# A hybrid attention and SSD layer on one core: the first phase in emission order, with the tokens' norms from squared rows

## The chip, the cores and the metric

The kernel runs on one core of one Trainium2 chip. A core has TensorE (matmuls), VectorE, ScalarE, GpSimd and SyncE; SyncE's queue (SP) issues every transfer of this kernel. The metric is the device time of one execution in microseconds (us), the median of several runs.

## The reference

One layer over 2048 tokens of 1024 features and 256 memory tokens, in float32:

```python
memn = rms_norm(mem, norm_mem_w)
hn = rms_norm(h, norm_in_w[layer])
proj = hn @ w_in[layer]
q, k, v, g_attn, z, xbc, dt_raw, q_mem, g_mem = jnp.split(proj, splits, axis=-1)
...                                   # rotary on q and k
att = window_attention(q, k, v, attn_sink[layer]).reshape(bsz, l, ATT_W)
...                                   # convolution, SSD scans in both directions, gate, norm
mkv = memn @ w_mem_kv[layer]
mk, mv = jnp.split(mkv, 2, axis=-1)
...                                   # attention of q_mem over mk, mv; gates
h = h + mixed @ w_out[layer]
return rms_norm(h, norm_out_w)        # rms_norm: y = x * rsqrt(mean(x*x) + 1e-6) * w
```

The first phase of the kernel, which the change edits, computes the memory's keys and values (`mkv`) and, for the last tokens, `hn` and from it `k` and `v`.

## The kernel before

Every float32 product is made from three matmuls of a faster 32-bit type: each operand is split into a high half (`xh`, `wh`, `memh`: a cast on ScalarE) and a low half (`xl`, `wl`, `meml`: a subtraction on VectorE, for a few tiles on GpSimd). `split3` issues high x high, high x low and low x high into one bank. A weight tile is 128 x 1024; `load_w` loads it into a staging tile `ws` (two buffers) and splits it into `wh` and `wl` (three buffers each).

The 2048 tokens are worked on in four chunks of 512, last chunk first, each with 128 tokens ahead of it, so 640 columns (`XW`). The first phase goes like this:

- memory: eight blocks of 128 features x 256 tokens are scaled and split (`memh`, `meml`). `mem_keys(hd, w)` makes the keys of one of four heads (24 matmuls of 256 columns); `mem_values(k2, w)` adds a quarter of the features to the values (12 matmuls of 512 columns) in two banks `pss`. The sums of squares go through `rstd_sq` (matmuls with a column of ones, then a power on GpSimd), `diag` (the norm of each token on a diagonal) and `rows_bc` (a matmul with ones, which spreads them over all rows; ScalarE copies the result).
- `mem_keys_out` multiplies keys by the norm (`kf`, VectorE), splits them into a tile "mk" and stores it in `mk_d`. The values are scaled from their banks, split (low half on GpSimd) into tiles "mk" too, and stored in `mv_d`. "mk" has two buffers.
- tokens: `xT` is loaded in eight blocks of 128 x 640. ScalarE squares them, VectorE adds the eight squares, `rstd_sq` sums them over the partitions. `prep_x` scales each block by weight and norm (VectorE), casts (ScalarE) and subtracts (VectorE).
- `keys` for the last chunk: two halves of 320 tokens. First both products with weight `wa` (banks `pa`), then for each half the product with `wb` (bank `pb`) and `rope`, in which VectorE multiplies `pa` and `pb` by the tables of `tables` (tile "tab", one buffer), adds, and ScalarE and VectorE split; two stores to `k_d`. Then `values`: five blocks of 24 matmuls of 272 columns. `pa`, `pb`, the blocks of `values` and the memory products share the three banks of `ps_pj`.

The order of instructions on TensorE is the order in which the program emits them. On the other engines and in SP's queue a scheduler orders them at compile time by readiness in its own model and by priority (`high_priority` raises it); each engine then runs its list in order, and an instruction that waits for a semaphore holds up all behind it. The lines that matter are L177 (all matmuls), L195 and L196 (cast and subtraction of `split`), L202 (weight loads), L361 (scaling of tokens), L371 (table), L862 and L864 (`kf` and its store), L241 to L243 (`rope`), L385 (store of keys), L850 (power) and L910:

```python
        for u in range(2):
            nc.sync.dma_start(mv_d[u, m], as32(mvs[u]))   # L910, m = 0 and 1; keys() comes next
```

## Time and profile before

| | |
|---|---|
| median of 3 runs | 1847.41 us (1845.33 to 1850.26) |
| the profiled execution's own time | 1848.8 us |
| its span, first to last instruction | 1847.1 us |
| TensorE busy, share of the span | 95% |
| mean granted clock of TensorE in it | 0.985 of full speed |

Times in the rows are us from the start of the span unless marked ns. A row of the waits says which engine and line waited for which, in total, how often and the longest. In a row of the timeline stand start, duration, engine, line, operation, output and inputs, and in brackets how long the engine sat idle before and until what. PEld is the loading of weights into TensorE, which overlaps PE, its matmuls.

### The profile page before, as it was taken

Reading aid. Unit: us, or ns where it says so; the run is one execution under the profiler, and the core shown is the slowest. Engines: PE = TensorE matmul, PEld = TensorE weight load, DVE = VectorE, ACT = ScalarE, POOL = GpSimd, SP = SyncE. Lnnn points to the kernel's source line nnn. Section 1 sums busy time; section 2 is a strip of 40 time slices with the busy share of each in tenths; the row PEclk is TensorE's granted clock in tenths of the full one; section 3 lists DMA queues with packets and bytes.
Section 4 is the critical chain, followed back from the end, with each engine's and each line's share of the span. In section 5 each row is a group of like instructions: output and inputs, shape, how many; then the busy total and the mean of one; then the engine's idle time right before and its main releaser. Section 6 shows DMA issues by size and latency. Waiting matters only on the chain. (4 is left out here: it accounts for less than half of the span.)

```text
span 1847.1 us, 26627 instructions
## 1 busy us (share of the span) xinstructions
PE 1755.7 (95%) x9242; PEld 1426.0 (77%) x9242; DVE 1179.9 (64%) x2681; ACT 921.4 (50%) x1985; POOL 260.3 (14%) x253
## 2 busy tenths in 40 slices
PE   7889999999799999999999989999998999999998
PEld 6878878877578787777778877778776777787886
DVE  7466666688576667778666777977677543443443
ACT  6237645664665566657555654656566411111121
POOL 1000000012200000121000002210111133333321
PEclk9989999999899999999999989999998999999999
DMA  7666364578653854776475466673658586566553
GB/s 237 211 197 187 123 214 146 152 241 244 210 169 122 268 165 150 240 245 206 142 211 161 133 205 195 190 214 118 197 179 265 165 251 182 164 180 180 171 176 120
DMA packets 264422, 347.59 MB, mean 188 GB/s; under 512 B 29536, under 2 KB 172000, under 8 KB 264288
## 3 DMA queue, kind: packets, MB, share of 16 engines
q1 hardware_dynamic: 264288, 345.90, 61.1%
q8 instruction: 73, 1.20, 0.3%
q14 instruction: 61, 0.50, 0.1%
HBM read 254.34 MB, written 91.49 MB: 187 GB/s over the span
## 5 line engine op out<-in xcount | busy, mean ns | idle before, releaser
L177 PE MATMUL pj<-xh,wh 128*128 128x512 f32 (+2 forms) x1296 | 506.6, 391 | 2.8 <-ACT xh L195 1.0
L177 PE MATMUL pj<-xl,wh 128*128 128x512 f32 (+2 forms) x1296 | 494.0, 381 | 4.8 <-DVE xl L196 4.8
L177 PE MATMUL pj<-xh,wl 128*128 128x512 f32 (+2 forms) x1296 | 494.7, 382 | 0.9 <-DVE wl L196 0.8
L196 DVE TENSOR_TENSOR wl<-ws,wh 128x1024 fp32r<-128x1024 f32 (+2 forms) x175 | 212.3, 1214 | 117.3 <-ACT wh L195 112.9
L177 PEld LDWEIGHTS pj<-xh,wl 128*128 128x128 f32 x1296 | 246.0, 190 | 46.9 <-DVE wl L196 2.7
L177 PEld LDWEIGHTS pj<-xh,wh 128*128 128x128 f32 x1296 | 246.7, 190 | 41.9 <-issue 3.7
L177 PEld LDWEIGHTS pj<-xl,wh 128*128 128x128 f32 x1296 | 246.8, 190 | 40.7 <-DVE xl L196 5.9
L195 ACT CAST wh<-ws 128x1024 fp32r<-128x1024 f32 (+2 forms) x175 | 180.0, 1029 | 179.3 <-PE pj L177 127.6
L546 DVE CUSTOM_DVE_ANT_0 pm<-s,band,sink 128x384 f32<-128x384 f32 (+1 forms) x256 | 150.3, 595 | 48.3 <-PE s L177 46.4
L554 ACT ACTIVATE pm<-pm,mx 128x385 f32<-128x385 f32 (+1 forms) x256 | 151.2, 595 | 55.5 <-DVE mx L552 55.5
L177 PE MATMUL pj<-woh,mxh 128*128 128x512 f32 x416 | 169.1, 407 | 0.0
L177 PE MATMUL pj<-woh,mxl 128*128 128x512 f32 x416 | 164.2, 395 | 0.0
L177 PE MATMUL pj<-wol,mxh 128*128 128x512 f32 x416 | 164.1, 394 | 0.0
L648 POOL TENSOR_TENSOR b<-nat,win 128x256 f32<-128x256 f32 x64 | 43.3, 697 | 841.2 <-ACT nat L632 841.2
L558 ACT ACTIVATE pm<-pm,den 128x384 f32<-128x384 f32 (+1 forms) x256 | 133.5, 595 | 6.9 <-DVE den L556 6.8
L572 ACT COPY pt<-t 128x512 f32<-128x512 f32 x120 | 69.4, 583 | 103.6 <-PE t L181 103.3
L195 ACT CAST mxh<-mxl 128x512 fp32r<-128x512 f32 x64 | 39.5, 617 | 162.8 <-DMA mxl<-mix_d 105.7
L181 PE MATMUL t<-ident,pm 128*128 128x128 f32 x736 | 103.8, 276 | 11.6 <-ACT nat L632 6.7
L181 PEld LDWEIGHTS t<-ident,pm 128*128 128x128 f32 x736 | 86.5, 142 | 34.6 <-ACT nat L632 7.6
L177 PE MATMUL s<-khh,qs 128*128 128x384 f32 (+1 forms) x256 | 94.7, 370 | 18.3 <-DVE mx L546 13.8
L484 DVE SCALAR_TENSOR_TENSOR cu<-raw,cw,cu 128x512 f32<-128x512 f32 (+2 forms) x128 | 99.3, 776 | 3.3 <-ACT cu L482 2.0
L177 PE MATMUL o<-pt,vg 128*64 128x256 f32 x736 | 93.8, 388 | 1.6 <-DVE dq L425 0.7
(222 smaller groups left out, 2842.8 us busy)
## 6 DMA issues: line engine op xcount, KB each, us to landing
ws<-in_w_in_dram SPq DMA_DIRECT2D x152, 512.0 KB, 4.2
q_d<-rt SPq DMA_DIRECT2D x32, 512.0 KB, 4.3
qs<-q_d SPq DMA_DIRECT2D x32, 512.0 KB, 6.1
fb<-f_d SPq DMA_DIRECT2D x32, 512.0 KB, 4.4
mxl<-mix_d SPq DMA_DIRECT2D x64, 256.0 KB, 4.1
mix_d<-ao SPq DMA_DIRECT2D x64, 128.0 KB, 3.5
xc<-xbc_d SPq DMA_DIRECT2D x32, 256.0 KB, 3.7
st_d<-carry SPq DMA_DIRECT2D x32, 256.0 KB, 3.9
```

The lines of the kernel that those rows point to most:

```text
L177: nc.tensor.matmul(out, lhsT=lhsT, rhs=rhs, start=start, stop=stop)
L181: nc.tensor.transpose(out, in_, ident)
L195: nc.scalar.copy(hi, x)
L196: (eng or nc.vector).tensor_tensor(lo, x, as32(hi), ALU.subtract)
L484: nc.vector.scalar_tensor_tensor(u, raw[:, r0 + k:r0 + k + cnt], cw[:, i, k:k + 1], u, ALU.mult, ALU.add)
L546: nc.vector.tensor_tensor_reduce(pm[:, r, :w], ss[:, :w], band[:, ms], 1.0, sink8[:, 4 * g + r:4 * g + r + 1], ALU.add, ALU.max, mx[:, r:r ...
L554: nc.scalar.activation(pm[:, r, :w + 1], pm[:, r, :w + 1], AF.Exp, bias=mx[:, r:r + 1], scale=0.125, accum_out=den[:, r:r + 1])
L558: nc.scalar.activation(pm[:, r, :w], pm[:, r, :w], AF.Copy, scale=den[:, r:r + 1])
L572: nc.scalar.copy(pts[j], tt)
L648: nc.gpsimd.tensor_tensor(xd[:, d], nat[:, 0:256].rearrange("p (r e) -> p r e", r=4), win[:, d, 4 * g:4 * g + 4].unsqueeze(2).broadcast_to ...
```

## The change

All edits but one helper's extra argument act on the first phase.

- `pin` queues an instruction behind the one that was emitted just before it on the same engine (or, for a transfer, in SP's queue). It is put on most ScalarE and VectorE instructions and on the loads of the first phase, the table's load among them, until `keys` for the last chunk has been emitted.
- `memT` is laid out by partition, in two parts of 128 rows of 1032 floats, with the memory's norm weights in the last 8. The small constants come as one tile `small` in one load.
- The first weights are loaded in a written order through four staging tiles: the two of "ws" and the tiles "rt0" and "rt1". The next four follow in the same tiles.
- The norms of the tokens come from rows: five blocks of 128 tokens x 1024 of `x` are loaded into `xall`, ScalarE squares each in place and sums it along the row (`accum_out`). Then `xT` is loaded over the same memory. The eight squares, seven additions and the sums over partitions of before go.
- The order of emission is new: `mem_values(1)` ahead of the memory's norm; the tokens' blocks in portions (`first_x`) between the weights of the later memory products; the weights of `keys` ahead of the last blocks; two of the three value weights inside `keys`. The low halves of token blocks 2 and 5 are subtracted on GpSimd. `mem_keys` of heads 0 and 2 uses the bank of `ps_o`.

```diff
+    starting = [True]
+    def pin(ins):
+        if starting[0]:
+            tc.keep_in_program_order(ins)
     def split(hi, lo, x, eng=None):
-        nc.scalar.copy(hi, x)
-        (eng or nc.vector).tensor_tensor(lo, x, as32(hi), ALU.subtract)
-    def load_w(src):
+        pin(nc.scalar.copy(hi, x))
+        i = (eng or nc.vector).tensor_tensor(lo, x, as32(hi), ALU.subtract)
+        if eng is None:
+            pin(i)
+    def load_w(src, ws=None):
         n = src.shape[-1]
         with tc.high_priority(offset=400):
-            ws = wsp.tile([P, D], F32, name="ws", bufs=2)
-            nc.sync.dma_start(ws[:, :n], src)
+            if ws is None:
+                ws = wsp.tile([P, D], F32, name="ws", bufs=2)
+                nc.sync.dma_start(ws[:, :n], src)
             wh = wsp.tile([P, D], F32R, name="wh")
             wl = wsp.tile([P, D], F32R, name="wl")
             split(wh[:, :n], wl[:, :n], ws[:, :n])
...
+    small = const.tile([P, 112], F32, name="small")
...
-        nc.sync.dma_start(cw, a["conv_w"])
         nc.vector.tensor_scalar(cw, cw, 0.5, None, ALU.mult)
-        nc.sync.dma_start(cb, a["conv_b"])
...
         for b in range(n):
-            nc.vector.tensor_scalar(dg[:, b * P:(b + 1) * P], ident, cols[:, b:b + 1], None, ALU.mult)
...
     def tables(t0, n):
         tab = misc.tile([P, 3, CH], F32, name="tab")[:, :, :n]
-        nc.sync.dma_start(tab, a["trig"][:, :, t0:t0 + n])
...
     dts = {}
...
-    def keys(c, xs):
+    def load_wv(j):
+        return load_w(a["w_v"][:, j * NV:min(j + 3, KT) * NV])
+    def keys(c, xs, ws=None):
         s, e = window(c)
-        wa, wb = load_w(a["w_in"][T_K]), load_w(a["w_in"][T_K + 1])
+        ahead = []
+        wa, wb = ws or [load_w(a["w_in"][T_K + u]) for u in range(2)]
         n = e - s if e - s <= CH else (e - s) // 2
         pas = yield from projs([(wa, o) for o in range(0, e - s, n)], xs, n)
         for o, pa in zip(range(0, e - s, n), pas):
             tab = tables(s + o, n)
+            if e == L and not o:
+                ahead = [load_wv(0), load_wv(3)]
             pb = yield from proj(wb, xs, o, n)
             for w, t in enumerate(rope(pa, pb, tab)):
                 nc.sync.dma_start(k_d[w, :, :, s + o:s + o + n], as32(t))
-    def values(c, xs):
+        return ahead
+    def values(c, xs, wv=()):
         s, e = window(c)
         nb = (e - s) // P
         if "task" in dts:
             need(dts["task"])
-        wv = [load_w(a["w_v"][:, j * NV:min(j + 3, KT) * NV]) for j in (0, 3, 6)]
+        wv = [*wv, *(load_wv(j) for j in (0, 3, 6)[len(wv):])]
...
-    nc.sync.dma_start(nwm, a["nw_mem"])
     memh = st_.tile([P, KT, MEM], F32R, name="memh")
     meml = st_.tile([P, KT, MEM], F32R, name="meml")
-    ms = [st_.tile([P, 4, MEM], F32, name="ms", bufs=2) for _ in range(2)]
+    ms = [st_.tile([P, 4 * MEM + KT], F32, name="ms", bufs=2) for _ in range(2)]
+    nwm = ms[0][:, 4 * MEM:]
+    def staging(src):
+        n = len(staged)
+        ws = (wsp.tile([P, D], F32, name="ws", bufs=2) if n % 4 < 2 else misc.tile([P, D], F32, name=f"rt{n % 4 - 2}"))
+        staged.append((src, ws))
+        return ws, src
+    staged = []
+    xall = st_.tile([P, KT * XW], F32, name="xall")
+    xraw = [xall[:, k * XW:(k + 1) * XW] for k in range(KT)]
+    x0 = window(NPER - 1)[0]
+    xss = misc.tile([P, 8], F32, name="ss", bufs=2)
+    msq = st_.tile([P, 4, MEM], F32, name="msq")
+    for out, src in ((ms[0], a["memT"][0]), staging(a["w_mk"][0]), (ms[1], a["memT"][1]), staging(a["w_mv"][0]),
+                     staging(a["w_mv"][1]), staging(a["w_mk"][1]),
+                     *((xall[:, b * D:(b + 1) * D], a["x"][x0 + b * P:x0 + (b + 1) * P, :]) for b in range(XW // P)),
+                     (small, a["small"])):
+        pin(nc.sync.dma_start(out, src))
+    def mem_tile(k):
+        x32 = ms[k // 4][:, (k % 4) * MEM:(k % 4 + 1) * MEM]
+        pin(nc.scalar.activation(memh[:, k], x32, AF.Copy, scale=nwm[:, k:k + 1]))
+        pin(nc.vector.scalar_tensor_tensor(meml[:, k], x32, nwm[:, k:k + 1], as32(memh)[:, k], ALU.mult, ALU.subtract))
+    def first_w(ws, n=1):
+        w = wsp.tile([P, D], F32R, name="wh"), wsp.tile([P, D], F32R, name="wl")
+        for o in range(0, D, D // n):
+            cs = slice(o, o + D // n)
+            pin(nc.scalar.copy(w[0][:, cs], ws[:, cs]))
+            pin(nc.vector.tensor_tensor(w[1][:, cs], ws[:, cs], as32(w[0])[:, cs], ALU.subtract))
+        return w
+    def x_squares(b):
+        xb = xall[:, b * D:(b + 1) * D]
+        pin(nc.scalar.activation(xb, xb, AF.Square, accum_out=xss[:, b:b + 1]))
+    mem_tile(0)
+    wk = [first_w(staged[0][1], 2)]
+    for k in range(1, KT):
+        mem_tile(k)
+    wv = [first_w(staged[1][1])]
+    msf = msq.rearrange("p j t -> p (j t)")
     for k2 in range(2):
-        nc.sync.dma_start(ms[k2], a["memT"][k2 * 512:(k2 + 1) * 512].rearrange("(j p) t -> p j t", p=P))
-        if k2 == 0:
-            wk = [load_w(a["w_mk"][0])]
-    wv = load_w(a["w_mv"][0])
-    nc.sync.dma_start(nw, a["nw_in"])
-    x0 = window(NPER - 1)[0]
-    xraw = [st_.tile([P, XW], F32, name="xraw", bufs=KT) for _ in range(KT)]
-    with tc.high_priority(offset=0):
-        for k in range(KT):
-            nc.sync.dma_start(xraw[k], a["xT"][k * P:(k + 1) * P, x0:])
-    msq = st_.tile([P, 4, MEM], F32, name="msq")
-    for k2 in range(2):
-        for j in range(4):
-            k = 4 * k2 + j
-            nc.scalar.activation(memh[:, k], ms[k2][:, j], AF.Copy, scale=nwm[:, k:k + 1])
-            nc.vector.scalar_tensor_tensor(meml[:, k], ms[k2][:, j], nwm[:, k:k + 1], as32(memh)[:, k],
-                                           ALU.mult, ALU.subtract)
+        sq = msf if k2 == 0 else ms[1][:, :4 * MEM]
+        pin(nc.scalar.activation(sq, ms[k2][:, :4 * MEM], AF.Square))
+    pin(nc.vector.tensor_tensor(msf, msf, ms[1][:, :4 * MEM], ALU.add))
+    for n in (2, 1):
+        pin(nc.vector.tensor_tensor(msq[:, :n], msq[:, :n], msq[:, n:2 * n], ALU.add))
+    wv.append(first_w(staged[2][1]))
+    wk.append(first_w(staged[3][1]))
+    for b in range(XW // P):
+        x_squares(b)
+    later = [staging(a[nm][n]) for nm, n in (("w_mv", 2), ("w_mk", 2), ("w_mv", 3), ("w_mk", 3))]
+    for out, src in (*later[:2], *((xraw[k], a["xT"][k * P:(k + 1) * P, x0:]) for k in range(4)), later[2],
+                     *((xraw[k], a["xT"][k * P:(k + 1) * P, x0:]) for k in range(4, KT)), later[3]):
+        pin(nc.sync.dma_start(out, src))
...
-        ps = bank(ps_pj, "pj")
+        ps = bank(ps_pj, "pj") if hd % 2 else bank(ps_o, "o")
...
-    nc.scalar.activation(msq, ms[0], AF.Square)
-    nc.scalar.activation(ms[1], ms[1], AF.Square)
-    nc.vector.tensor_tensor(msq, msq, ms[1], ALU.add)
-    for n in (2, 1):
-        nc.vector.tensor_tensor(msq[:, :n], msq[:, :n], msq[:, n:2 * n], ALU.add)
-    xsq = misc.tile([P, XW + 6], F32, name="raw", bufs=2)[:, :XW]
-    for k in range(KT):
-        sq = xsq if k == 0 else misc.tile([P, XW], F32, name="th", bufs=2)
-        nc.scalar.activation(sq, xraw[k], AF.Square)
-        if k:
-            nc.vector.tensor_tensor(xsq, xsq, sq, ALU.add)
     pss = [bank(ps_pj, "pj") for _ in range(2)]
-    def mem_values(k2, w=None):
-        wh, wl = w or load_w(a["w_mv"][k2])
+    def mem_values(k2, w):
+        wh, wl = w
         for m in range(2):
             yield from split3(pss[m], [(mh[2 * k2 + j][:, m * P:(m + 1) * P], ml[2 * k2 + j][:, m * P:(m + 1) * P],
                                         wh[:, j * 512:(j + 1) * 512], wl[:, j * 512:(j + 1) * 512])
                                        for j in range(2)], start=k2 == 0, stop=k2 == 3)
     pk = main(mem_keys(0, wk[0]))
-    main(mem_values(0, wv))
+    main(mem_values(0, wv[0]))
+    main(mem_values(1, wv[1]))
     mcol = rstd_sq(msq[:, 0], 2)
     nc.vector.tensor_scalar(vcol, mcol[:, :2], 0.5, None, ALU.mult)
-    main(mem_values(1))
+    pin(nc.vector.tensor_scalar(xss[:, :XW // P], xss[:, :XW // P], 1.0 / D, EPS, ALU.mult, ALU.add))
+    nc.gpsimd.tensor_tensor(xss[:, :XW // P], xss[:, :XW // P], neghalf[:, :XW // P], ALU.pow)
     rows_bc(diag(mcol, 2), 2, mrow)
     mem_keys_out(0, pk)
-    xcol = rstd_sq(xsq, XW // P)
-    main(mem_values(2))
-    mem_keys_out(1, main(mem_keys(1, load_w(a["w_mk"][1]))))
+    pk = main(mem_keys(1, wk[1]))
+    mem_keys_out(1, pk)
     rb = st_.tile([P, XW], F32, name="rb")
-    with tc.high_priority(offset=200):
-        rows_bc(diag(xcol, XW // P), XW // P, rb)
-        xs = prep_x(NPER - 1, rb, xraw)
-    mem_keys_out(2, main(mem_keys(2, load_w(a["w_mk"][2]))))
-    main(mem_values(3))
-    mem_keys_out(3, main(mem_keys(3, load_w(a["w_mk"][3]))))
+    xs = [], []
+    def first_x(ks):
+        todo = []
+        for k in (*ks, None):
+            if k is not None:
+                x32 = misc.tile([P, XW], F32, name="xp", bufs=4)
+                pin(nc.vector.scalar_tensor_tensor(x32, xraw[k], nw[:, k:k + 1], rb, ALU.mult, ALU.mult))
+                for t, nm in zip(xs, ("xh", "xl")):
+                    t.append(xhl.tile([P, XW], F32R, name=nm))
+                pin(nc.scalar.copy(xs[0][k], x32))
+                todo.append((k, x32))
+            while todo and (k is None or len(todo) > 1):
+                q, x32 = todo.pop(0)
+                if q % 3 == 2:
+                    nc.gpsimd.tensor_tensor(xs[1][q], x32, as32(xs[0][q]), ALU.subtract)
+                else:
+                    pin(nc.vector.tensor_tensor(xs[1][q], x32, as32(xs[0][q]), ALU.subtract))
+    dg = diag(xss, XW // P)
+    w = load_w(*staged[4])
+    rows_bc(dg, XW // P, rb)
+    main(mem_values(2, w))
+    first_x((0,))
+    w = load_w(*staged[5])
+    first_x((1, 2))
+    mem_keys_out(2, main(mem_keys(2, w)))
+    w = load_w(*staged[6])
+    first_x((3, 4, 5))
+    main(mem_values(3, w))
+    w = load_w(*staged[7])
+    wkey = [load_w(a["w_in"][T_K + u]) for u in range(2)]
+    first_x((6, 7))
+    mem_keys_out(3, main(mem_keys(3, w)))
     small_constants()
     for m in range(2):
         mv = msq[:, 2 * m:2 * m + 2].rearrange("p j t -> p (j t)")
@@ -909,8 +969,9 @@
         for u in range(2):
             nc.sync.dma_start(mv_d[u, m], as32(mvs[u]))
-    main(keys(NPER - 1, xs))
-    main(values(NPER - 1, xs))
+    wv = main(keys(NPER - 1, xs, wkey))
+    starting[0] = False
...
-        "xT": f(x0.T), "x": f(x0), "memT": f(mem0.T), "mem": f(mem0),
+        "xT": f(x0.T), "x": f(x0), "memT": f(np.concatenate([ktp(mem0.T).reshape(P, 2, 4 * MEM).transpose(1, 0, 2),
+                                  np.broadcast_to(nwm, (2, P, KT))], 2)), "mem": f(mem0),
```

## Rows read from the trace of the kernel before

**Rows 1.** The page, busy us (share of the span) and instructions of the engines.

```profile
PE 1755.7 (95%) x9242; PEld 1426.0 (77%) x9242; DVE 1179.9 (64%) x2681; ACT 921.4 (50%) x1985; POOL 260.3 (14%) x253
```

**Rows 2.** Timeline of TensorE: first of `keys`, last stretch of `keys`, first of `values`, first after.

```profile
44.29 0.31 PE L177 MATMUL pj<-xh,wh 128*128 128x320 f32 x1
...
59.00 0.31 PE L177 MATMUL pj<-xh,wh 128*128 128x320 f32 x1
...
65.16 0.29 PE L177 MATMUL pj<-wh,xh 128*128 128x272 f32 x1
...
83.55 0.39 PE L177 MATMUL pj<-xh,wh 128*128 128x512 f32 x1
```

**Rows 3.** Waits of TensorE up to 84: us in total, times, longest.

```profile
PE pj L177 <- ACT memh L835: 8.9, 1, 8.9
PE pj L177 <- DVE wl L196: 3.1, 1, 3.1
PE t L177 <- DVE msq L870: 2.9, 1, 2.9
```

**Rows 4.** Windows: stretch, length, busy us (instructions) by engine, granted clock, DMA share, GB/s.

```profile
8.90:14.50 5.60, 5.59 (x24) 5.36 (x25) 3.97 (x10) 5.60 (x12) 0.00 (x0) 1.00 1.03 394
...
20.40:25.40 5.00, 5.00 (x17) 3.75 (x17) 4.29 (x12) 1.01 (x3) 1.35 (x1) 0.66 0.94 319
...
34.00:39.90 5.90, 5.85 (x36) 5.01 (x36) 3.75 (x5) 2.80 (x6) 0.00 (x0) 1.00 0.57 176
...
44.20:52.70 8.50, 5.33 (x34) 4.54 (x32) 8.50 (x13) 5.33 (x9) 0.00 (x0) 0.97 0.42 129
```

**Rows 5.** Timeline of SP, GpSimd and VectorE: last stores of the memory, a table, its reader.

```profile
54.52 0.33 SPq L864 DMA_DIRECT2D mk_d<-mk  x1
...
58.60 1.89 POOL L196 TENSOR_TENSOR mk<-msq,mk 128x512 fp32r<-128x512 f32 x1 [27.88 <-DMA mk_d<-mk]
...
62.66 1.30 POOL L196 TENSOR_TENSOR mk<-msq,mk 128x512 fp32r<-128x512 f32 x1 [2.17 <-DMA mv_d<-mk]
...
64.36 0.56 SPq L371 DMA_DIRECT2D tab<-in_trig_dram  x1
...
68.53 0.82 DVE L241 TENSOR_TENSOR xp<-pj,tab 128x640 f32<-128x640 f32 x1 [2.27 <-DMA tab<-in_trig_dram]
```

**Rows 6.** Timeline of the start: the first load and the casts of the first two weights.

```profile
0.80 0.39 SPq L202 DMA_DIRECT2D ws<-in_w_mk_dram  x1
...
4.38 1.04 ACT L195 CAST wh<-ws 128x1024 fp32r<-128x1024 f32 x1 [2.31 <-DMA ws<-in_w_mk_dram]
...
5.81 1.05 ACT L195 CAST wh<-ws 128x1024 fp32r<-128x1024 f32 x1 [0.38 <-DMA ws<-in_w_mv_dram]
```

**Rows 7.** Timeline of the norms: GpSimd's power, x's column sums, x's diagonals.

```profile
23.40 1.35 POOL L850 TENSOR_TENSOR ss<-ss,neghalf 128x2 f32<-128x2 f32 x1 [20.49 <-DVE ss L849]
...
25.92 1.17 PE L177 MATMUL t<-ones,raw 128*128 128x1 f32 x10
...
30.76 1.07 DVE L311 TENSOR_SCALAR th<-ident,ss 128x128 f32<-128x128 f32 x5 [0.47 <-POOL ss L850]
```

**Rows 8.** Groups by shape up to 84: count, busy us, mean ns, idle before, releasers.

```profile
L196 DVE TENSOR_TENSOR wl<-ws,wh 128x1024 fp32r<-128x1024 f32 x11 | 13.5, 1223 | 17.5 <-ACT wh L195 17.5
L195 ACT CAST wh<-ws 128x1024 fp32r<-128x1024 f32 x12 | 12.5, 1046 | 12.1 <-DMA ws<-in_w_mk_dram 5.2 <-PE pj L177 4.4 <-DMA ws<-in_w_mv_dram 1.9
...
L361 DVE SCALAR_TENSOR_TENSOR xp<-xraw,nw,rb 128x640 f32<-128x640 f32 x8 | 6.8, 880 | 0.0
L196 DVE TENSOR_TENSOR xl<-xp,xh 128x640 fp32r<-128x640 f32 x8 | 6.3, 820 | 0.0
...
L862 DVE TENSOR_TENSOR kf<-pj,gm 128x256 f32<-128x256 f32 x4 | 1.7, 420 | 0.0
```

**Rows 9.** Timeline of the rotary's sum on VectorE and its stores.

```profile
62.70 1.94 DVE L243 TENSOR_TENSOR xp<-xp 128x640 f32<-128x640 f32 x1
...
66.62 1.24 SPq L385 DMA_DIRECT2D k_d<-xp  x2
```

More of the change, by code (lines that the diff above doesn't have):

```diff
@@ L266, in layer @@
     nc.vector.memset(neghalf, -0.5)
-    nw = const.tile([P, KT], F32, name="nw")
-    nwm = const.tile([P, KT], F32, name="nwm")
-    cw = const.tile([P, 8, 5], F32, name="cw")
-    cb = const.tile([P, 8], F32, name="cb")
-    dsk = const.tile([P, 4], F32, name="dsk")
-    snw = const.tile([P, 4], F32, name="snw")
-    sink = const.tile([P, 16], F32, name="sink")
+    small = const.tile([P, 112], F32, name="small")
+    nw, cb, dsk, snw = (small[:, o:o + n] for o, n in ((0, 8), (8, 8), (16, 4), (20, 4)))
+    cw = small[:, 24:64].rearrange("p (i k) -> p i k", i=8)
+    sink, dtb, aneg = (small[:, o:o + 16] for o in (64, 80, 96))
     sink8 = const.tile([P, 16], F32, name="sink8")
-    dtb = const.tile([P, 16], F32, name="dtb")
-    aneg = const.tile([P, 16], F32, name="aneg")
     dcy = const.tile([P, NB, 2, 8], F32, name="dcy")
@@ L310, in diag @@
         for b in range(n):
-            nc.vector.tensor_scalar(dg[:, b * P:(b + 1) * P], ident, cols[:, b:b + 1], None, ALU.mult)
+            pin(nc.vector.tensor_scalar(dg[:, b * P:(b + 1) * P], ident, cols[:, b:b + 1], None, ALU.mult))
         return dg
@@ L319, in rows_bc @@
             mm(ps[:, :m], ones, dg[:, b * P:b * P + m], True, True)
-            nc.scalar.copy(out[:, b * P:b * P + m], ps[:, :m])
+            pin(nc.scalar.copy(out[:, b * P:b * P + m], ps[:, :m]))
     def window(c):
@@ L350, in norm_x, with prep_x @@
             nc.sync.dma_start(xn_d[kt, :, s:s + w], x32)
-    def prep_x(c, rb=None, raw=None):
+    def prep_x(c):
         s, _ = window(c)
@@ L357, in prep_x @@
             x32 = misc.tile([P, XW], F32, name="xp", bufs=4)[:, :w]
-            if raw is None:
-                nc.sync.dma_start(x32, xn_d[kt, :, s:s + w])
-            else:
-                nc.vector.scalar_tensor_tensor(x32, raw[kt], nw[:, kt:kt + 1], rb[:, :w], ALU.mult, ALU.mult)
+            nc.sync.dma_start(x32, xn_d[kt, :, s:s + w])
             xh = xhl.tile([P, XW], F32R, name="xh")
@@ L848, in rstd_sq @@
         with tc.high_priority(offset=300):
-            nc.vector.tensor_scalar(ss[:, :nblk], pn[:, :nblk], 1.0 / D, EPS, ALU.mult, ALU.add)
+            pin(nc.vector.tensor_scalar(ss[:, :nblk], pn[:, :nblk], 1.0 / D, EPS, ALU.mult, ALU.add))
             nc.gpsimd.tensor_tensor(ss[:, :nblk], ss[:, :nblk], neghalf[:, :nblk], ALU.pow)
@@ L861, in mem_keys_out @@
         kf = st_.tile([P, MEM], F32, name="kf")
[L862 removed]
+        pin(nc.vector.tensor_tensor(kf, ps, mrow, ALU.mult))
         split(mk[:, :MEM], mk[:, MEM:], kf)
         nc.sync.dma_start(mk_d[hd], as32(mk))
[L866 to L876 removed]
     pss = [bank(ps_pj, "pj") for _ in range(2)]
[L879 to L880 removed]
+    def mem_values(k2, w):
+        wh, wl = w
         for m in range(2):
@@ L910, in layer @@
             nc.sync.dma_start(mv_d[u, m], as32(mvs[u]))
-    main(keys(NPER - 1, xs))
-    main(values(NPER - 1, xs))
+    wv = main(keys(NPER - 1, xs, wkey))
+    starting[0] = False
+    main(values(NPER - 1, xs, wv))
     rx.close()
@@ L1097, in prepare @@
     xo = np.concatenate([n * 128 + np.arange(128) for n in (0, 1, 4, 6, 2, 3, 5, 7)])
+    nwm = np.asarray(norm_mem_w).reshape(KT, P).T
     pos = np.arange(L, dtype=np.float32)
@@ L1108, in prepare @@
         "w_out": f(wo[rows]),
-        "nw_in": f(np.asarray(norm_in_w)[0].reshape(KT, P).T),
-        "nw_mem": f(np.asarray(norm_mem_w).reshape(KT, P).T),
         "nw_out": f(norm_out_w),
-        "sink": f(np.asarray(attn_sink)[0]),
-        "conv_w": f(np.asarray(conv_w)[0][:, xo].T.reshape(8, P, 5).transpose(1, 0, 2)),
-        "conv_b": f(np.asarray(conv_b)[0][xo].reshape(8, P).T),
-        "dt_bias": f(np.asarray(dt_bias)[0].reshape(16)),
-        "a_log": f(np.asarray(a_log)[0].reshape(16)),
-        "d_skip": f(np.repeat(np.asarray(d_skip)[0], 64).reshape(4, P).T),
-        "ssd_norm": f(np.asarray(ssd_norm_w)[0].reshape(4, P).T),
+        "small": f(np.concatenate([
+            np.asarray(norm_in_w)[0].reshape(KT, P).T,
+            np.asarray(conv_b)[0][xo].reshape(8, P).T,
+            np.repeat(np.asarray(d_skip)[0], 64).reshape(4, P).T,
+            np.asarray(ssd_norm_w)[0].reshape(4, P).T,
+            np.asarray(conv_w)[0][:, xo].T.reshape(8, P, 5).transpose(1, 0, 2).reshape(P, 40),
+            *(np.broadcast_to(np.asarray(v).reshape(16), (P, 16)) for v in (attn_sink[0], dt_bias[0], a_log[0]))], 1)),
         "trig": f(np.stack([-tbl(np.sin), tbl(np.cos), tbl(np.sin)], 1)),
```

7 lines of the change are left out of this document (1 added, 6 removed).

## The prediction

> **What bounds the kernel now.** I read the page's busy times first, to see who sets the end. TensorE is busy 95% of the span [rows 1], so what the first phase loses or wins reaches the end almost whole. The edits lie in that phase, which for TensorE ends with the last matmul of `values` for the last chunk, at 83.55 [rows 2]. Second, TensorE's own waits up to there: 8.9 us before the first matmul, 3.1 for a late low half of a value weight, 2.9 for the sums of the memory's squares [rows 3]. Third, the windows, to see what stands behind the waits: from 44.2 to 52.7 VectorE is busy 8.50 of 8.50 us and TensorE 5.33, and after an earlier wait the granted clock is 0.66 over 20.4 to 25.4, a mix of the levels of 1.2 and 2.4 GHz [rows 4]. VectorE, then, is what TensorE waits for when tokens are prepared. Last I followed the timeline of the stores of `mem_keys_out` and of the memory values, because the change queues a load behind them [rows 5].
>
> **The start.** `memT` now leads SP's queue, in rows as long as those of the weight that led it before. That one was issued at 0.80 and its cast began at 4.38; the next 512 KB let a cast begin at 5.81 [rows 6]. So the first memory block is scaled at 4.4, half of the weight is cast from 5.8, and TensorE starts near 6.5 instead of 8.9. Its first product took 5.6 for 24 matmuls, against about 2.8 later (36 matmuls of a key and a value product take 5.85) [rows 4]; I keep 5.6.
>
> **To the norms.** Before, the key products 0 and 1, the value products 0 to 2 and the matmuls of both norms were done when `mem_keys(2)` started, at 34.0 [rows 4]: 25.1 after the first matmul, 2.9 of it the wait for the squares [rows 3]. After, 22.2 of work less 1.2 for the ten column sums of x [rows 7]. New waits: value product 1 now stands ahead of the memory's norm, so nothing covers the norm's way through a column sum, VectorE, GpSimd's power of 1.35 [rows 7], the diagonals and back: 2.4. Value product 1's low half of its weight comes behind two squares and three adds: 1.1. The five diagonals of x, 1.07 [rows 7], are emitted behind `mem_keys_out(1)`, which is a product, a cast and a subtraction of some 0.4 each: 2.4. The sum is 6.5 + 21.0 + 5.9 = 33.4; up to 1.5 falls away if the slow spell at 20.4 [rows 4] doesn't come back. I take 33.0, so the early start is nearly used up. ScalarE's five row squares, each about a cast of 1024 [rows 8], run under TensorE's first products, and the 2.6 MB of rows ride behind the weights. They cost nothing while the last square ends (near 20.5) before the memory's norm does (21.5); each us beyond that delays the x diagonals by one.
>
> **VectorE up to the keys.** Value product 2 takes the last 2.8 of that, so the low half of its weight is there at 30.2. From then VectorE has, in emission order, six scalings of 0.88, four subtractions of 0.82, three weights of 1.22 and `mem_keys_out(2)` with 0.84 [rows 8]: 13.1 busy, and about 2.5 of waits, once for the copies of the norm's rows and otherwise for a cast that itself waits for VectorE. The last memory weight is done at 45.8. Before, the tokens were prepared beside these products and inside `keys`, where they cost 6.8 of its 20.9 (44.29 to 65.16, against 96 matmuls of 0.147 [rows 2]). Two of the eight subtractions go to GpSimd. A 640-wide sum on VectorE took 1.94 while GpSimd had one of 1.30 [rows 5, 9], against 0.82 for such widths otherwise [rows 8]. So each can cost VectorE between nothing and 1.1; one of the two is counted with 1.1, the other falls into a wait of VectorE.
>
> The Trainium skill's page "SBUF — State Buffer", section "Who interferes with whom", says that a VectorE instruction with two SBUF inputs and a GpSimd one that reads SBUF shut each other out, the second waiting for the whole of the first. The trace agrees in kind, with 1.12 lost beside an instruction of 1.30 [rows 5, 9]; by the page both subtractions would be paid whole, and the sum would be some 2 us later than by the row.
>
> `mem_keys(3)` then needs 2.6 more, and `keys` starts at 45.8 + 1.1 + 2.6 = **49.5**, against 44.29.
>
> **Keys and values.** Without waits `keys` takes 96 x 0.147 = 14.1 (42 matmuls from 59.00 to 65.16) and `values` 15.1 (65.16 to 83.55, less 3.3 waited) [rows 2]. The stalls of before inside them, 6.8 and 3.3, go, as the tokens and the early value weights are ready. But `tables` is now pinned, and a pinned transfer stands in SP's queue behind the transfer emitted before it. For the first half that is the last store of the memory values. The two buffers of "mk" chain that store: the low half of values 0 on GpSimd waits until the store of head 3 has landed, the low half of values 1 until the store of the first has. Before: store at 54.52, GpSimd at 58.60 and 62.66, a table issued behind it at 64.36, its first reader at 68.53 [rows 5]; that was the second half's table, the first half's had come long before. After, the product of head 3 stands on VectorE behind two key weights and token blocks 6 and 7 (2.44 + 1.76 + 1.64 [rows 8]), which is 3.1 after `keys` starts. From it 1.4 to its store, then 4.1, 1.6 (GpSimd), 2.1, 1.3, 0.4, 4.2 as in the rows [rows 5] and 0.8 for the reader: 15.9. The first bank is free at 49.5 + 3.1 + 15.9 = 68.5. The second half's `pb`, fourth user of three banks, could start 10.6 after `keys`, at 60.1. **Wait: 8.4.**
>
> The second half's table stands behind the first half's two `k_d` stores. From `pb`'s start 0.8 for the other rotary product, 3.9 from the sum to the stores (62.70 to 66.62 [rows 9]), 1.2 to issue them, 4.2 to land the table, 0.8 to read: 10.9, until a bank is free for block 1 of `values`. `pb` and block 0 cover 3.5 + 3.0. **Wait: 4.4**, which also hides a slow spell after the first one. The last four blocks take 12.1, so the phase ends at 68.5 + 10.9 + 12.1 = **91.5** instead of 83.55: 8.0 later. Behind it nothing is edited; the loads of single constants that go weren't waited for by TensorE [rows 3].
>
> The profiled execution took 1848.8 (span 1847.1, 1.7 around it), so the sum is 1856.8; the median of the runs is 1.4 below that execution, so I forecast **1855.4**.
>
> **Bounds.** The first wait loses 2 if head 3's store lands as fast as that of the values (2.1) and gains 2 if that one is as slow as head 3's (4.1). VectorE without its 2.5 and 1.1 takes 3.6 off, a slow spell of TensorE in each gap adds 2 to 4. Together: 1850 to 1861.
>
> **Rivals.** (1) *The table is not late.* If it has landed 9.8 after `keys` starts, the waits on it shrink to about 1 in all, and the phase ends at 49.5 + 29.2 + 1 = 79.7: 3.9 earlier, **1843.5**. For it: the first half's table of before came far ahead. Against it: it was issued 9.8 after head 3's store [rows 5], where SP waited in order. (2) *VectorE keeps up too*, and tokens are ready when TensorE asks. Then TensorE has 6.5 + 5.6 + 7 x 2.8 + 2.5 for the norms' matmuls + 4.8 of norm waits = 39, + 29.2 + 1 = 69: **1833**. It decides once the low halves of weights don't stand behind scalings; 13.1 of VectorE against 8.5 of TensorE in that stretch speak against it. (3) *Both GpSimd subtractions hold VectorE for their whole length*, 1.30 x 640/512 = 1.6 each: 3.2 instead of 1.1, **1857.5**. The one overlap in the rows, 1.12, is nearly of that size. The lock that the Trainium skill describes is this case.
>
> **How the numbers follow.** 0.3% is 5.5 us, about what this kernel's runs can tell from no change; it lies at 1852.9 and 1841.9. The forecast gets 0.60, seven tenths of it above 1852.9; (1) 0.20, half of it below 1841.9; (2) 0.10; (3) 0.10. Slower: 0.42 + 0.10 = 0.52; same: 0.18 + 0.10 = 0.28; faster: 0.10 + 0.10 = 0.20. The range holds the forecast, (3) and most of (1): 1840 to 1862; the forecast's own is 1850 to 1861.
>
> **What would show it.** TensorE's first matmul near 6.5. Between 33 and 50 its waits for low halves of memory weights, with VectorE full. `keys` from about 49.5 without a wait for a token block. Then SP standing at a store of the memory values with the table behind it, VectorE's first rotary product waiting for that table, and TensorE idle some 8 us inside `keys` and 4 inside `values`. The forecast is wrong if the table lands before `pb` of the second half is due, or if `keys` starts by 44.

## The result, and the profile after

The changed kernel took 1860.39 us (median of 6 runs), the kernel before in the same runs 1850.28 (6 runs): a ratio of 1.0063 with a 95% interval of 1.0046 to 1.0080, so slower by 0.6%. In a second group of runs (a0, below) the ratio was again 1.0063. The profiled execution took 1863.33 us, its span is 1861.6. The time lies in the predicted range, on the side that had the largest chance, 5 us above the forecast value.

TensorE's waits up to 90 us of the changed kernel answer to [rows 3]. The columns are us in total, times and the longest.

```profile
PE pj L177 <- DVE xp L252: 6.8, 2, 6.5
PE o L177 <- ACT wh L851: 6.7, 1, 6.7
PE s L177 <- DVE th L310: 3.9, 2, 2.2
PE pj L177 <- ACT wh L202: 2.8, 2, 1.9
PE pj L177 <- DVE wl L203: 2.0, 2, 1.3
PE pj L177 <- DVE wl L852: 1.2, 1, 1.2
```

The wait for the squares is gone and the first matmul comes 2.3 earlier. In their place stand two waits for diagonals (`th`), some for the high and low halves of weights, and one of 6.5 for the first rotary product, line 252. The next view is the timeline around that wait: SP, GpSimd, VectorE and TensorE, answering to [rows 5].

```profile
53.86 0.33 SPq L905 DMA_DIRECT2D mk_d<-mk  x1
...
56.09 1.29 POOL L203 TENSOR_TENSOR mk<-msq,mk 128x512 fp32r<-128x512 f32 x1 [10.05 <-DMA mk_d<-mk]
59.62 1.40 POOL L203 TENSOR_TENSOR mk<-msq,mk 128x512 fp32r<-128x512 f32 x1 [2.23 <-ACT wh L202]
...
61.05 0.32 SPq L970 DMA_DIRECT2D mv_d<-mk  x1
61.91 0.33 SPq L213 DMA_DIRECT2D ws<-in_w_in_dram  x1
62.30 0.67 SPq L367 DMA_DIRECT2D tab<-in_trig_dram  x1
...
67.67 0.82 DVE L252 TENSOR_TENSOR xp<-pj,tab 128x640 f32<-128x640 f32 x1 [5.63 <-DMA tab<-in_trig_dram]
...
68.64 0.61 PE L177 MATMUL pj<-xh,wh 128*128 128x320 f32 x1 [6.52 <-DVE xp L252]
```

Read from the top: the store of head 3 lands, GpSimd makes the two low halves of the memory values, the last of their stores leaves at 61.05, only then is the first half's table asked for, VectorE stands idle for it, and TensorE stands behind VectorE. (The row at 59.62 names a ScalarE cast that ended in that moment. The store of the first low half, issued at 57.41, took 2.1 to land and so ended just before it; its buffer is the one that GpSimd writes next.) The last view is the windows (busy us and instructions of PE, PEld, DVE, ACT, POOL, then the granted clock).

```profile
33.00:50.98 17.98, 12.24 (x60) 9.93 (x61) 15.28 (x18) 9.83 (x14) 3.15 (x2) 0.84 0.25 82
50.98:58.00 7.02, 7.02 (x46) 7.02 (x46) 2.38 (x5) 2.23 (x5) 1.29 (x1) 0.93 0.36 132
58.00:70.00 12.00, 5.48 (x34) 5.25 (x33) 5.48 (x7) 1.59 (x3) 1.40 (x1) 0.82 0.60 197
70.00:89.52 19.52, 19.25 (x141) 19.03 (x140) 5.45 (x8) 5.49 (x13) 0.00 (x0) 0.94 0.70 215
```

Up to the keys (33.00 to 50.98) VectorE is busy 15.28 of 17.98 us and TensorE 12.24. In the stretch with the table (58.00 to 70.00) TensorE does 5.48 us of work in 12. The first matmul behind `values` comes at 89.52 instead of 83.55 [rows 2]: 6.0 of the 10.1 us are lost in the edited phase.

### The profile page after: what moved, and what is told of

Same layout as the page of the kernel before. It is cut to its first block, busy times and chain, and to the rows that moved or that the text cites. A ratio compares the mean times of both kernels' runs of the same rounds, so it can differ in the third digit from the quotient of the medians.

```text
span 1861.6 us, 26597 instructions
## 1 busy us (share of the span) xinstructions
PE 1759.1 (94%) x9232; PEld 1427.8 (77%) x9232; DVE 1181.1 (63%) x2673; ACT 921.5 (49%) x1988; POOL 262.1 (14%) x255
## 4 chain that ended last, share of the span: by engine, by line
PE 63%; DMA 13%; DVE 10%; ACT 8%; issue 3%; POOL 2%; SPq 1%; POOLq 0%; DVEq 0%; ACTq 0%
PE pj L177 46%; PE s L177 7%; PE o L177 6%; PE t L181 5%; ACT pm L557 2%; DVE wl L203 2%; DMA mix_d<-b 2%; DMA mxl<-mix_d 1%; DMA xn_d<-xp 1%; ACT pm L561 1%; DMA b<-y_d 1%; DMA cu<-in_x_dram 1%; ACT wh L202 1%; DVE pm L549 1%; DMA fb<-ef_d 1%
## 5 line engine op out<-in xcount | busy, mean ns | idle before, releaser
L203 DVE TENSOR_TENSOR wl<-ws,wh 128x1024 fp32r<-128x1024 f32 (+2 forms) x169 | 206.4, 1223 | 117.9 <-ACT wh L202 107.6
L202 ACT CAST wh<-ws 128x1024 fp32r<-128x1024 f32 (+2 forms) x169 | 173.6, 1029 | 166.4 <-PE pj L177 126.8
L487 DVE SCALAR_TENSOR_TENSOR cu<-raw,small,cu 128x512 f32<-128x512 f32 (+2 forms) x128 | 99.7, 779 | 3.8 <-ACT cu L485 2.6
L203 DVE TENSOR_TENSOR mxl<-mxl,mxh 128x512 fp32r<-128x512 f32 x64 | 51.0, 798 | 75.9 <-ACT mxh L202 75.6
```

The costliest lines, as they stand in the source:

```text
L202: pin(nc.scalar.copy(hi, x))
L203: i = (eng or nc.vector).tensor_tensor(lo, x, as32(hi), ALU.subtract)
L487: nc.vector.scalar_tensor_tensor(u, raw[:, r0 + k:r0 + k + cnt], cw[:, i, k:k + 1], u, ALU.mult, ALU.add)
```

## The experiments

Each kernel was timed against the kernel before in the same group of runs, whose median was 1851.1 (a0, e1, e2, e4), 1853.8 (e3, e5, e7, e8), 1854.9 (e6, e9, e10) and 1851.8 (e11). "Phase" is the first matmul behind `values` in the one profiled execution, less the 83.55 of before, "run" the median less before's of the group, "rest" their difference. The two rows of the unedited change differ by 1.4 in the rest, so no rest is known better than that.

```
       what it is                           phase   run    ratio (95%)              rest
after  the change                            +6.0  +10.1   1.0063 (1.0046, 1.0080)  +4.1
a0     the change again                      +5.3  +10.8   1.0063 (1.0047, 1.0080)  +5.5
e1     change, tables unpinned               -0.1   +5.9   1.0030 (1.0014, 1.0046)  +6.0
e3     change, both tables early             -3.5   +0.7   1.0003 (0.9987, 1.0019)  +4.2
e4     change, weights before tokens         +4.1   +9.4   1.0055 (1.0041, 1.0070)  +5.3
e5     change, GpSimd's share on VectorE     +5.0   +8.0   one run                  +3.0
e6     e3 and e4                             +5.1   +9.1   1.0062 (1.0039, 1.0086)  +4.0
e7     change, ten tiny matmuls first        +7.6   +6.8   1.0032 (1.0017, 1.0047)  -0.8
e8     e1, ten tiny matmuls first            -3.4   -2.8   0.9985 (0.9967, 1.0002)  +0.6
e9     e3, ten tiny matmuls first            -3.2   -5.0   0.9978 (0.9963, 0.9994)  -1.8
e11    e3, 42 tiny matmuls first             -4.2   -2.4   0.9980 (0.9967, 0.9992)  +1.8
e2     before, tables placed as changed      +8.4   +6.5   1.0038 (1.0023, 1.0052)  -1.9
e10    before, inputs packed as changed      -1.1   -4.2   0.9976 (0.9963, 0.9988)  -3.1
```

**Is it the table's place? e1, e2 and e3.** The theory is that the table's place in SP's queue is what the phase pays for; the rival, VectorE's longer chain ahead of the keys.

```diff
 e1 (changed kernel)
-        pin(nc.sync.dma_start(tab, a["trig"][:, :, t0:t0 + n]))
+        nc.sync.dma_start(tab, a["trig"][:, :, t0:t0 + n])
 e2 (kernel before; the first half's table is also asked for ahead of the keys' weights)
-        nc.sync.dma_start(tab, a["trig"][:, :, t0:t0 + n])
+        ld = nc.sync.dma_start(tab, a["trig"][:, :, t0:t0 + n])
+        if starting[0]:
+            tc.keep_in_program_order(ld)
 e3 (changed kernel, behind the later loads)
+    n = XW // 2
+    tabs = [tables(x0, n), st_.tile([P, 3, n], F32, name="tb")]
+    pin(nc.sync.dma_start(tabs[1], a["trig"][:, :, x0 + n:x0 + 2 * n]))
```

> The changed kernel with one line undone: the loads of the two rotary tables are no longer held in emission order, so that the first half's table is asked for at the start and only the second half's stands behind the stores of the memory values. Theory (the table's place in SP's queue is the price): the 6.5 us wait of the second half's product of the second key weight goes, it starts near 62 instead of 68.6, the slow clock behind the wait goes with it, and the values end at 81.5 to 84 instead of 89.5; the run is 6 to 8 us faster than the changed kernel, which is about the time before. Rival (VectorE's longer chain ahead of the keys is the price): the keys still start at 51, the wait moves from the table to VectorE's own work, and the run gains under 2 us.

> The kernel before with only the place of the two tables' loads taken from the change: the first half's behind the last store of the memory values, the second half's behind the first half's key stores. Theory (this alone costs what the change costs): the keys start at 44.3 as before, but the second half's product of the second key weight waits until the table has come (SP frees at 64, so VectorE reads it at 67 and TensorE starts at 68 to 69, a wait of 7 to 9 us), the values end at 88 to 90 instead of 83.6, and the run is 4 to 9 us slower than before. Rival (the table is covered, the changed VectorE order makes the loss): under 2 us slower.

> The changed kernel with both rotary tables asked for behind the last memory weight's load and the token blocks', ahead of every store of the memory's results (the second one into a tile of its own). Theory: the first half's wait is gone as in the run with the tables unpinned (e1), and so is the 1.9 us that TensorE still waits there for the second half's first rotary product, whose table stands behind the memory values' last store; the values end about 2 us earlier than in e1, near 80, and the run is 1 to 3 us faster than e1. Rival (that wait covers one that VectorE's splits would cause anyway): the same as e1 within 1 us.

In e1 the keys started at 51.74, no earlier than in the changed kernel, and the phase ended at 83.45 instead of 89.52. The run was 5.0 us faster than a0, less than the 6 to 8 expected. From the keys on, TensorE's one wait was for the second half's table, still behind the stores:

```profile
70.41 0.82 DVE L252 TENSOR_TENSOR xp<-pj,tab 128x640 f32<-128x640 f32 x1 [2.77 <-DMA tab<-in_trig_dram]
...
71.29 0.39 PE L177 MATMUL pj<-wh,xh 128*128 128x272 f32 x1 [1.93 <-DVE xp L252]
```

e3 took that wait too. The phase ended at 80.02, with the first matmul behind `values`, and the run was level with before (+0.7), 2.6 us faster than e1 in the medians, 5.2 against before of each group, where 1 to 3 was expected:

```profile
80.02 0.39 PE L177 MATMUL pj<-xh,wh 128*128 128x512 f32 x1
```

e2 put the wait into the kernel before:

```profile
65.52 0.32 SPq L915 DMA_DIRECT2D mv_d<-mk  x1
65.89 0.68 SPq L373 DMA_DIRECT2D tab<-in_trig_dram  x1
...
70.08 0.82 DVE L241 TENSOR_TENSOR xp<-pj,tab 128x640 f32<-128x640 f32 x1 [4.38 <-DMA tab<-in_trig_dram]
...
71.05 0.60 PE L177 MATMUL pj<-xh,wh 128*128 128x320 f32 x1 [8.45 <-DVE xp L241]
```

The same chain, a wait of 8.45, and 6.5 us on the whole run. Not all of its 8.4 us of phase is the table's, though: its keys started at 46.75 where 44.3 was expected, so 2.5 were lost ahead of them, for a reason not shown, and from the keys' start to the phase's end it took 5.9 more than before. The theory holds for the phase. The order of two loads is worth 9.5 us of phase between the changed kernel and e3, and without it the change's first phase is 3.5 us shorter than before. The run of e1, though, stayed 5.9 us slower than before with a phase that is not. That part is the rest, below.

**Would an earlier start of the keys help? e4 and e6.** Both split the last three memory weights ahead of the token blocks; e6 has e3's tables too.

```diff
     main(mem_values(2, w))
-    first_x((0,))
     w = load_w(*staged[5])
-    first_x((1, 2))
     mem_keys_out(2, main(mem_keys(2, w)))
...
+    first_x((2,))
     mem_keys_out(3, main(mem_keys(3, w)))
+    first_x((3, 4, 5))
+    wkey.append(load_w(a["w_in"][T_K + 1]))
+    first_x((6, 7))
```

> The changed kernel with the emission order of the splits changed: the last three memory weights are split ahead of the token blocks instead of between them, and the two key weights between the blocks; the tables stay where the change puts them. If VectorE's chain makes the keys late, their first matmul comes at 44 to 46 instead of 51.0, but VectorE's work is the same in sum, so that token blocks then feed the keys' first product (waits of 0.5 to 2 us inside it). If the store of the memory values behind ScalarE and GpSimd sets the end, the phase ends 3 to 5 us earlier, since those stores move up with the last memory product, and the run is 3 to 5 us faster than the changed kernel; if they do not move, the second half's wait on the table only grows by what the keys gain, and the run is the same within 1 us.

> Both tables early (e3) and the memory weights' splits ahead of the token blocks (e4). With the table out of the way the keys' start should count: e4 ended the phase 2.4 us ahead of the changed kernel although its table still stood behind the stores, so the phase ends 2 to 4 us ahead of e3 and the run is 2 to 4 us faster than e3, 1850 to 1852. Rival (the token blocks are then late inside the keys' first product and take it back): within 1 us of e3.

The keys did start at 45.23 and 46.94, but e4 gained 1.5 us of run on a0, which their intervals can't tell from nothing, and e6 missed altogether: 8.4 us slower than e3 against before, with its phase ending at 88.66, about where e4's did (87.63). In e4, too, TensorE waits 6.2 us for token blocks and no longer for the table. TensorE's waits for token blocks in e6 from 46 to 70, and the two windows behind the keys' start, first of e6:

```profile
PE pj L177 <- ACT xh L942: 2.8, 2, 1.9
PE pj L177 <- DVE xl L949: 2.3, 3, 1.3
PE pj L177 <- POOL xl L947: 1.2, 1, 1.2
```

```profile
45.00:57.00 12.00, 8.47 (x46) 6.99 (x45) 9.70 (x10) 6.66 (x10) 3.50 (x3) 0.85 0.35 121
57.00:69.00 12.00, 8.77 (x39) 8.03 (x39) 8.59 (x8) 3.29 (x5) 3.12 (x2) 0.73 0.35 105
```

and of e3:

```profile
45.00:57.00 12.00, 10.73 (x67) 10.52 (x66) 7.67 (x9) 4.74 (x8) 1.64 (x2) 0.86 0.35 114
57.00:69.00 12.00, 12.00 (x88) 11.88 (x87) 8.42 (x13) 4.38 (x8) 2.15 (x1) 1.00 0.76 235
```

TensorE started sooner on data that was no sooner ready: it waits for token blocks six times, 6.3 us in all, and the granted clock is 0.85 and then 0.73, mixes of its two levels of 1.2 and 2.4 GHz. e3 starts its keys 3.6 us later and from 57 runs 12.00 of 12.00 us at full clock. Late and whole beats early and in pieces.

**What does GpSimd's share cost VectorE? e5.**

```diff
-                if q % 3 == 2:
+                if False:
```

> The changed kernel with the two token blocks' low halves that GpSimd computes put back on VectorE. If GpSimd's subtractions lengthen VectorE's rows beside them by as much as the prediction counted (1.1 us for one), VectorE's chain up to the first matmul of the keys grows by 2 x 0.82 less 2 x 1.1, so that the keys start within 0.6 us of where they do; if by the 0.5 us that one row showed, they start about 1.1 us later (52.1). If VectorE stood still for the whole of GpSimd's 1.5 us each, they start 1.4 us earlier. The span stays within 1 us in every case, since the table sets when the second half goes on.

The row of the last memory weight, first in the changed kernel (a0) beside GpSimd's subtraction, then in e5:

```profile
43.73 1.57 POOL L944 TENSOR_TENSOR xl<-xp,xh 128x640 fp32r<-128x640 f32 x1 [6.14 <-ACT xh L939]
...
44.63 1.75 DVE L203 TENSOR_TENSOR wl<-rt,wh 128x1024 fp32r<-128x1024 f32 x1 [1.00 <-ACT wh L202]
```

```profile
44.92 1.23 DVE L203 TENSOR_TENSOR wl<-rt,wh 128x1024 fp32r<-128x1024 f32 x1
```

It ends at 46.38 and at 46.15 (in the first profile of the changed kernel at 47.13): moving two of eight subtractions to GpSimd bought nothing that shows, since VectorE then waits 1.00 for ScalarE and its row is 0.52 longer. The other of the two, from 36.03 to 37.58 in a0, lengthened no row: beside it VectorE mostly waited or multiplied a bank's values by the norm, in the usual 0.42. The keys of e5 started at 51.07, against 50.23 in a0 and 50.98 in the changed kernel's first profile. The expectation had 52.1 for the 0.5 us of loss; it left out the wait of 1.00. (One run of e5 was taken.) By the Trainium skill's page "SBUF — State Buffer", section "Who interferes with whom", VectorE's two-input instruction and GpSimd's shut each other out; the trace agrees for these two rows, which overlap for 0.67 us, VectorE's being 0.52 longer.

**Where does the rest come from? a0, e10, e7, e8, e9, e11.** Behind the phase TensorE's list is the same in all kernels. The windows behind it, of before and of the change, show what the 8.5 us more there are made of in these two profiles: TensorE is busy 2.6 us longer, at a lower granted clock, and idle 5.9 us longer.

```profile
83.55:1847.10 1763.55, 1691.76 (x8864) 1367.53 (x8862) 1128.19 (x2597) 882.24 (x1922) 252.37 (x239) 0.99 0.61 187
89.52:1861.60 1772.08, 1694.38 (x8864) 1369.70 (x8862) 1134.26 (x2597) 882.09 (x1922) 252.11 (x239) 0.98 0.61 186
```

First, the change once more, and the change's packing alone in the kernel before:

```diff
 e10 (kernel before)
-    nw = const.tile([P, KT], F32, name="nw")
...
+    small = const.tile([P, 112], F32, name="small")
...
-        nc.sync.dma_start(ms[k2], a["memT"][k2 * 512:(k2 + 1) * 512].rearrange("(j p) t -> p j t", p=P))
+        nc.sync.dma_start(ms[k2], a["memT"][k2])
-    nc.sync.dma_start(nw, a["nw_in"])
+    nc.sync.dma_start(small, a["small"])
```

> The changed kernel once more, unedited, for a second profile beside the first. In the first, the offset of its TensorE stream against the kernel before was about +6 us at the end of the first phase and grew to +14 by the end of the span. If the later growth belongs to the new order of the unedited stages, the same waits recur at the same places (4.35 us near 975 us, on loads of xT that reach VectorE late) and the span lies again 13 to 15 us above before's. If it belongs to one execution, the first-phase offset recurs (+5.5 to +6.5) and the later jumps fall elsewhere, with a span 8 to 12 us above.

> The kernel before with only the change's packing of inputs: the small vectors as one tile loaded at once, the memory laid out by partition with its norm weight behind it. Its first phase otherwise keeps before's order. All eight profiles with the changed kernel's packing show an offset against before that grows by 5 to 10 us behind the first phase; the one profile without the packing (e2) grew by 1.2. Theory (the packing itself costs late: other places of the tensors in memory, seven loads fewer in SP's list): the phase ends within 1 us of before or earlier, the offset then grows by 5 us or more, the weight loads land in about 4.45 us in the mean instead of 4.3, and the run is 3 to 7 us slower than before. Rival (the growth follows what the first phase hands on, or chance): growth within 2 us and the run within 2 us of before.

a0 repeated a wait of 3.60 near 974, and its offset to the profile of before again grew, to 14 us. The packing alone is cleared, and more: it makes the kernel faster, by 0.24% with an interval wholly below 1. In its profile the stretch behind the phase is 3.6 us longer than in the profile of before, but its runs aren't slower: the profiled execution of before, at 1848.8, is itself 2 to 6 us below the later medians of before, so offsets to one profile overstate the rest. I go by medians from here. The next theory was TensorE's code. In a0 an instruction packet is on the DMA engines between 941.5 and 943.5 (the view by DMA queue), and in that moment SP takes 1.58 us to issue a load (its timeline):

```profile
q8 instruction: 1, 0.02, 4.2%
```

```profile
941.75 1.58 SPq L213 DMA_DIRECT2D ws<-in_w_in_dram  x1
...
974.49 0.69 PE L177 MATMUL s<-khh,qs 128*128 128x384 f32 x1 [3.60 <-DVE mx L549]
```

That they are TensorE's is worked out from the traces: the queue has 73 packets of 16 KB in an execution, TensorE 18,675 instructions, so 256 to a packet, and in the two profiles of the changed kernel most packets come within 12 instructions of the same place in TensorE's list. The change has 19 instructions fewer on TensorE than before. So instructions were put back, where TensorE has nothing to do (e7; e8 and e9 the same in e1 and e3):

```diff
         ps = bank(ps_pj, "pj") if hd % 2 else bank(ps_o, "o")
+        for _ in range(10 if hd == 0 else 0):
+            nc.tensor.matmul(ps[:, :1], lhsT=ones, rhs=ones[:, 0:1], start=True, stop=True)
 e11: 42 of them, with lhsT=ones[:, 0:1]
```

> The changed kernel with ten one-column matmuls more (20 instructions with their weight loads) in TensorE's idle time ahead of its first matmul, so that TensorE has as many instructions as in the kernel before (18694 against 18675) and each 16 KB block of its code is fetched at the matmul at which it is fetched there. Theory (the late growth of the offset comes from code blocks of TensorE that now arrive on the DMA engines in the middle of SP's issues): the fetch at 941.6 moves to 938, the 1.58 us issue of a weight load there falls back to 0.37, the wait near 970 shrinks from 3.6 to about 2 us, the clock stays at 1.0 behind it, the offset between 280 us and the end grows by 0 to 3 us instead of 8, and the run is 4 to 7 us faster than the changed kernel. Rival (the growth comes from elsewhere, as from where tensors lie in memory): the growth is again 7 to 8 us and the run within 1.5 us of the changed kernel.

> The same ten one-column matmuls in the kernel whose tables are unpinned (e1). Theory of the code blocks: 4 to 7 us faster than e1, so 1850 to 1853, level with the kernel before or up to 1 us faster. Rival: within 1.5 us of e1.

> Both tables early (e3) and the ten one-column matmuls ahead of the first product. In e8 these kept the granted clock of 12 to 24 us at 1.00 where e1 had 0.91 and the phase ended 3 to 4 us earlier; e3 without them already had 1.00 there. If the clock of that stretch is what they bought, they add under 1.5 us to e3; if they also save in later stages, the run is 4 us or more faster than e3, about 1850.

> Both tables early (e3) with 42 one-column, one-row matmuls ahead of the first product in place of e9's ten one-column ones. In the traces each such fp32 matmul is two matmuls and two weight loads, so the ten added 40 instructions and these add 168: TensorE is as busy ahead of its first product, but its 16 KB code blocks fall half a block (128 instructions) from where they fall in e9. The three kernels with the ten matmuls ran 4.6 to 8 us faster than the same kernels without them, measured against before in the same runs. If where the code blocks fall is what they bought, this run is not like e9: it loses some or all of those 4.6 us, towards e3's ratio of 1.000. If a busy TensorE at the start bought it, it is like e9: ratio 0.996 to 0.999. If the difference of e3 and e9 was chance between groups of runs, it lies anywhere between the two.

Each of these matmuls is two in the trace, so that ten add 40 instructions and not the 20 that the expectations of e7 and e8 count with. In e7 the packet came before that load's issue, which fell back to 0.37:

```profile
948.52 0.33 SPq L507 DMA_DIRECT2D q_d<-rt  x1
948.96 0.37 SPq L213 DMA_DIRECT2D ws<-in_w_in_dram  x1
```

but the wait behind it stayed at 3.6, against the expectation. The runs did get faster against before, by 0.31% (e7 against a0), 0.45% (e8 against e1) and 0.25% (e9 against e3), each from another group of runs than the kernel that it is set against; the intervals of e9 and e3 overlap. e11, whose code lies half a block elsewhere, gained about what e9 did, 0.23%. That speaks against the place of the code blocks, and so does a count of SP's issues over 0.9 us: 24 in the profile of before, 28 in a0, but 28 in e7 and 32 in e11 as well.

What the table shows is that the rest is +3.0 to +6.0 in the seven rows with the changed start and TensorE idle for its first 6.4 to 7.1 us, and -1.8 to +1.8 in the four where tiny matmuls fill some of that time. Idleness at the start can't be all of it: e2 and e10 are idle for 8 us there and have rests of -1.9 and -3.1. Nor do the profiles show the gain: behind the phase the four with tiny matmuls take 5 to 13 us longer than the profile of before, as the others with the changed start do (5 to 11). Single executions of one kernel differ by up to 17 us. The granted clock goes with the runs: its mean is 0.980 over the twelve runs of the change and 0.983 over the fourteen of before in a0's group, while e9 and e11 have that of before in theirs (0.983 and 0.984). Whether that is cause or consequence isn't shown. How work in the first 5.5 us acts on later stages stays open, and with it this part of the cause. Three versions beat both kernels, e9, e10 and e11, by 0.20 to 0.24% against before.

## Why the prediction was right, and where it was not

**The start and the norms** came out as summed: first matmul 6.65 (forecast 6.5), waits for the diagonals 1.70 and 2.20 (2.4 and 2.4), for the value weight's low half 1.18 (1.1), and the slow spell came back.

**VectorE up to the keys:** the keys started at 50.98 instead of 49.5, but VectorE was only 0.2 late. Its chain was the right one, and the last memory weight was done at 47.13, with 46.9 forecast: its waits, most of them for ScalarE, came to 4.0 instead of 2.5, GpSimd cost 0.52 instead of 1.1, and the chain began 0.4 earlier. The term that was too small is the last memory product behind it: 3.80 instead of 2.6. TensorE had waited for both halves of that weight, and its granted clock over the product is 0.67, a mix of the two levels. Row and window:

```profile
45.38 1.75 DVE L203 TENSOR_TENSOR wl<-rt,wh 128x1024 fp32r<-128x1024 f32 x1 [1.00 <-ACT wh L202]
```

```profile
47.18:50.98 3.80, 3.80 (x22) 3.80 (x23) 3.80 (x4) 1.37 (x3) 0.00 (x0) 0.67 0.42 116
```

**The first wait:** the mechanism was right, and e2 shows it alone. The second half went on at 68.64 (forecast 68.5), but that so exact an end came out is luck: from head 3's store to GpSimd took 2.2 instead of 4.1, while the table was asked for 1.3 after GpSimd's last row instead of 0.4, behind a weight load, and was read 5.4 after that instead of 4.2. The wait was 6.5 instead of 8.4, since the keys started 1.5 later against the same end and their products ahead of it took 0.5 longer.

**The second wait was mis-sized:** 0.27 instead of 4.4. The stores were issued 2.2 after the second product's start instead of 4.7. The 3.9 from sum to stores that [rows 9] show held two things that did not come back: the sum took 0.83, not the 1.94 beside GpSimd, and in the kernel before SP stood 1.1 us at a load of the memory values, which waited for their store to land, ahead of those stores. The prediction did not see that. So the whole chain was 8.7 instead of 10.9 long, and with that the phase cost 6.0 instead of 8.0. The product's first 3.6 us ran at the clock's lower level, with matmuls 0.27 apart instead of 0.15, and so covered most of what was left of the wait. The load in the kernel before, then the sum, the stores, the wait and the slow stretch in the changed one:

```profile
66.19 0.38 SPq L691 DMA_DIRECT2D mvt<-mv_d  x1
```

```profile
69.26 0.83 DVE L254 TENSOR_TENSOR xp<-xp 128x640 f32<-128x640 f32 x1
...
70.87 1.38 SPq L387 DMA_DIRECT2D k_d<-xp  x2
...
77.36 0.39 PE L177 MATMUL pj<-wh,xh 128*128 128x272 f32 x1 [0.27 <-DVE xp L252]
```

```profile
68.64:72.24 3.60, 3.60 (x13) 3.60 (x14) 2.24 (x3) 0.72 (x1) 0.00 (x0) 0.50 0.03 11
```

**"Behind it nothing is edited"** failed: 4 to 5.5 us were lost there without an edited line. The prediction put that stretch at nothing, and why it isn't stays open. The forecast of 1855.4 is right in direction and in the mechanism of the phase. That it is only 5 off is in part luck: 2 too much in the phase stands against 4 to 5.5 too little behind it, and the median of before had moved up by 2.9.

**Rival (1)** gave a phase end of 79.7 for a table that isn't late: e3 measured 80.02, with keys 1.1 later and no wait where 1 was counted. Its 1843.5 us would still have been wrong, because of the rest. **Rival (2)** fails in e6: reordering brings the keys forward, not the tokens. **Rival (3)** fails in the rows beside e5: 0.52 lost for one subtraction, nothing for the other.

## What to carry to other kernels

Pinning a transfer into emission order makes it wait for every store ahead of it in SP's queue; a load that depends on nothing belongs ahead of the first store that waits for compute. Before an engine is made to start earlier, look at whether its last input is earlier too: here the pieces with waits between them also ran at a lower clock (0.73 in e6). And a phase that ends earlier in one profile isn't yet a faster kernel; compare its gain with the medians, whose difference may come from stages that nobody edited.

## What the runs showed that was not expected

An instruction packet on the DMA engines coincided with a slow issue on SP: 1.58 us, against 0.37 for the same load in e7, where the packet came earlier. It is no rule, but more than chance: in a0, 69 of SP's 1067 issues meet one of the 73 packets in time, and 18 of its 28 issues over 0.9 us are among them. The Trainium skill's page "Runtime: NRT & Kernel Launch", section "Instruction fetch mechanics", says that code comes in blocks of 16 KiB and that the cost of crossing into the next is mostly hidden. The trace agrees on the blocks, 73 packets of 16 KB; for the cost to TensorE itself no run here shows a number. And ten matmuls that compute nothing, placed where TensorE was idle, went with runs that are 0.25 to 0.45% faster against before; why, is open.
